# Conformer layer on one core: a sixth channel tile convolved by taps, statistics taken over pairs of tiles

## The chip, the core and the metric

The kernel runs on one NeuronCore of a Trainium2 chip. The core has TensorE (PE; its weight loads are listed apart as PEld), VectorE (DVE), ScalarE (ACT), GpSimd (POOL) and SyncE (SP, which here issues every transfer). Each engine works through a queue of its own in order; between engines there are only semaphores. The metric is the device time of one execution in microseconds.

## The reference, cut to what matters

A trunk of two layers over 512 positions and 1024 channels, all in float32. Layer 0 mixes by a gated DeltaNet, layer 1 by a Conformer convolution; both then attend to a memory of 256 positions and end in a squared-ReLU MLP. The change touches layer 1's mixer:

```python
def conformer_conv(h, w_pw1, b_pw1, w_dw, b_dw, ln_g, ln_b, w_pw2, b_pw2):
    u = h @ w_pw1 + b_pw1
    u = u[..., :D_MODEL] * jax.nn.sigmoid(u[..., D_MODEL:])
    c = causal_depthwise_conv(u, w_dw) + b_dw          # width 31, each channel by itself
    c = jax.nn.silu(layer_norm(c, ln_g, ln_b))         # mean and variance over the 1024 channels
    return c @ w_pw2 + b_pw2
```

`h` comes in after an RMS normalisation, and the result is added to the residual.

## The kernel before, in words

**Layout.** Activations lie with 128 channels on the partitions and 512 positions along the row: eight channel tiles, m = 0 to 7. Products are made at float32 precision from three matmuls: each operand is split into a high part (rounded by a copy on ScalarE) and the rest (a subtraction).

**Weights.** They come in units of 128 x 1024 (`raw`, loaded by SP into one of three buffers). `wsplit` casts a unit on ScalarE (`wh`, L207) and subtracts (`wl`, L70) on VectorE, or on GpSimd for all of pw1 and for every other unit of this layer's K and V. The split pair has three buffers, so the cast of unit u waits until TensorE is done with unit u - 3. In the Conformer layer I number the units: 0 to 15 are pw1 (two for each channel tile), 16 to 31 the K and V projections of the memory for the attention that follows (placed here as filler for TensorE, with their own high and low parts `Kh`, `Kl`, `Vh`, `Vl` and the scaled `kf`), 32 on pw2. Each unit of pw1 and pw2 is 24 matmuls of 128x512, each of K 24 of 128x256, each of V 12 of 128x512.

**Gate.** For each tile m, `pw_ev` scales the two halves of pw1's result by the RMS factor (`sg`, `pa` on VectorE), takes the sigmoid on ScalarE, and multiplies: `xp` for tile 0, `x` for tiles 1 to 4, `glu` for tiles 5 to 7.

**Convolution, in three ways.** In the program before:
- tile 0 by taps on GpSimd and ScalarE (`pool_conv`): for each of 31 taps ScalarE makes the product with the tap's weight (`cvp`, one or two instructions, L1052 and L1054, since positions are stored by phase of four) and GpSimd adds it to the accumulator (`ca<-ca,cvp`);
- tiles 1 to 4 by taps on VectorE (`dve_conv`): one multiply-add per tap on an accumulator in PSUM (`ca<-x,prm,ca`, 30 for each tile), after which ScalarE copies the accumulator to SBUF (L1072);
- tiles 5, 6 and 7 on TensorE (`conv`): the gated tile is rearranged by 16 small transfers on SP (`xg`), and 36 matmuls against nine prepared matrices of diagonals (`tap`, loaded by `taps`) give the result with positions on the partitions; VectorE adds it to `cy`, which holds the bias.

Tiles convolved by taps are turned by four transposes on TensorE (`turn`, `cvT`) and copied to `Y` (`cy`) by ScalarE.

**Normalisation.** `bn_stats` on VectorE takes the statistics of every tile and row block (32 instructions, of the transposes' PSUM or of `cy`), `bn_aggr` joins them, ScalarE takes the root, VectorE the reciprocal and the scaling of the eight `cy` tiles (L79). `ln_out` turns each tile back (`lnT`, four transposes), applies Silu on ScalarE (`la`) and splits it (`lsh` on ScalarE, `lsl` on VectorE). pw2 follows.

**Order.** `CONV_SEQ` lists the 32 units; behind each, some taps are taken from the lists of VectorE and GpSimd (`taps_dve`, `taps_pool`), and `CONV_AFTER` names what follows which unit: "t" loads diagonals, "c" convolves on TensorE, "d" turns a tile, "l" normalises, "o" writes a tile out. What the loop records is then ordered by a scheduler, engine by engine, so an instruction can stand elsewhere in its queue than the loop alone says; the order that results is fixed when the program is built, and can be read from it.

Of the kernel before, what the change touches and what calls it, by code (L numbers as in the profile page):

```python
# [8 lines left out]
F32 = mybir.dt.float32  # L9
F32R = mybir.dt.float32r  # L10
AF = mybir.ActivationFunctionType
ALU = mybir.AluOpType
# [1 line left out]

P = 128
NT = 512
NTAP = 5
KT = 8
EPS = 1e-6
LN_EPS = 1e-5  # L20
# [9 lines left out]
OFF["w_tap"] = _o  # L30
_o += NTAP * 31
OFF["out_norm"] = _o
# [6 lines left out]
def tile_trunk(ctx, tc, xT, memT, prm_d, adt_d, bdw_d, tap_d, fin_d, w_ab, w_kq, w_v, w_z, w_dno, w_pw1, w_pw2,  # L39
               w_q, w_k, w_vv, w_o, w_up, w_dn, yT):  # L40
    nc = tc.nc
    pe, act, dve, pool = nc.tensor, nc.scalar, nc.vector, nc.gpsimd
# [2 lines left out]
    wp = ctx.enter_context(tc.tile_pool(name="wp", bufs=2))  # L45
    fsp = ctx.enter_context(tc.tile_pool(name="fsp", bufs=3))
    up = ctx.enter_context(tc.tile_pool(name="up", bufs=NSLOT))
    sp = ctx.enter_context(tc.tile_pool(name="sp", bufs=13))
    psp = ctx.enter_context(tc.tile_pool(name="psp", bufs=8, space=bass.MemoryType.PSUM))

    cnt = [0]
# [5 lines left out]
    def slot(dt=F32, s="u", shape=(P, NT)):  # L57
        return up.tile(list(shape), dt, tag="u", name=nm(s))
# [7 lines left out]
    def const(shape, s, dt=F32):  # L66
        return cp.tile(list(shape), dt, tag=s, name=s)
# [67 lines left out]
    eps_ln = const([P, 1], "eps_ln")  # L135
# [128 lines left out]
    def split(src, s):  # L264
        h = slot(F32R, s + "h")
        act.copy(h, src)
        lo = slot(F32R, s + "l")
        tt(dve, lo, src, h.bitcast(F32), ALU.subtract)
        return h, lo
# [721 lines left out]
    def taps(m):  # L991

        TAPS[m] = []
        for i in range(9):
            t = slot(s="tap")
            nc.sync.dma_start(out=t, in_=tap_d[m - NTAP, i])
            TAPS[m].append(t)

    def conformer(norm, hres, nxt):
        xs = norm.xs  # L1000
        st, xg = {}, {}
        bn = slot(s="bn")
        Y = [[slot(s="cy") for _ in range(2)] for _ in range(4)]
# [7 lines left out]
        def pw_ev(m):  # L1011
            sg = slot(s="sg")
            tt(dve, sg, st.pop((m, 1)), norm.rb, ALU.mult)
            act.activation(sg, sg, AF.Sigmoid, bias=pc("b_pw1", 8 + m))
            a = slot(s="pa")
            tt(dve, a, st.pop((m, 0)), norm.rb, ALU.mult)
            if m == 0:
                x4 = c4(wp.tile([P, 544], F32, tag="cv", name=nm("xp"), bufs=NCV))
                pool.memset(x4[:, :, 0:8], 0.0)
                stt(x4[:, :, 8:136], c4(a), pc("b_pw1", m), c4(sg), ALU.add, ALU.mult)  # L1020
                todo_p.extend(pool_conv(m, x4))
                return
            if m < NTAP:
                x7 = fsp.tile([P, 1024], F32, tag="fs", name=nm("x7"))[:, 0:1008].rearrange("p (q t) -> p q t", q=7)
                pool.memset(x7[:, :, 0:10], 0.0)
                stt(x7[:, 3:7, 8:136], c4(a), pc("b_pw1", m), c4(sg), ALU.add, ALU.mult)
                act.copy(x7[:, 0:3, 9:137], x7[:, 4:7, 8:136])
                todo.extend(dve_conv(m, x7))
                return
            x = wp.tile([P, 544], F32, tag="cv", name=nm("xg"), bufs=NCV)  # L1030
            x4 = c4(x)
            pool.memset(x4[:, :, 0:8], 0.0)
            gl = slot(s="glu")
            stt(gl, a, pc("b_pw1", m), sg, ALU.add, ALU.mult)
            for j in range(4):
                for b in range(4):
                    nc.sync.dma_start(out=x4[32 * b:32 * b + 32, j, 8:136],
                                      in_=gl[32 * j:32 * j + 32, 128 * b:128 * b + 128])
            xg[m] = x4

        todo, todo_p, acc = [], [], {}
# [17 lines left out]
        def dve_conv(m, x7):  # L1059
# [13 lines left out]

            return [lambda d=d: tap(d) for d in range(31)]

        def taps_pool(n):
            for _ in range(min(len(todo_p), n)):
                todo_p.pop(0)()

        def taps_dve(us):  # L1080
            for _ in range(min(len(todo), round(us * TAP_RATE))):
                todo.pop(0)()

        def turn(m):
            ps = psum("cvT")
            for r in range(4):
                pe.transpose(ps[:, r * P:(r + 1) * P], acc[m][:, r * P:(r + 1) * P], ident)
            del acc[m]
            for r in range(4):
                y = ps[:, r * P:(r + 1) * P]  # L1090
                act.copy(Y[r][m // 4][:, m % 4 * P:m % 4 * P + P], y)
                dve.bn_stats(out=bn[:, (r * 8 + m) * 6:(r * 8 + m) * 6 + 6], in_=y)

        def conv(m, js):
            if js[0] == 0:
                st["cv", m] = psum("cv")
            ps = st["cv", m]
            for j in js:
                o = ps[:, j * P:(j + 1) * P]
                for u in range(9):  # L1100
                    x = xg[m][:, j, 8 - u:136 - u]
                    if u < 8:
                        pe.matmul(o, x, TAPS[m][2 * j + u // 4][:, (u % 4) * P:(u % 4 + 1) * P],
                                  start=u == 0, stop=False)
                    else:
                        pe.matmul(o[:, 0:64], x, TAPS[m][8][:, j * P:j * P + 64], start=False, stop=True)
            if js[-1] == 3:
                del TAPS[m], xg[m]
                ps = st.pop(("cv", m)).rearrange("p (j r c) -> p j r c", j=4, r=4)
                for r in range(4):  # L1110
                    y = Y[r][m // 4][:, m % 4 * P:m % 4 * P + P]
                    y3 = y.rearrange("p (j c) -> p j c", j=4)
                    tt(dve, y3, ps[:, :, r, :], y3, ALU.add)
                    dve.bn_stats(out=bn[:, (r * 8 + m) * 6:(r * 8 + m) * 6 + 6], in_=y)

        def ln():
            mv = small(8, "mv")
            for r in range(4):
                dve.bn_aggr(out=mv[:, 2 * r:2 * r + 2], in_=bn[:, r * 48:r * 48 + 48])
            v = mv.rearrange("p (r k) -> p r k", k=2)  # L1120
            sd = small(4, "lsd")
            act.activation(sd, v[:, :, 1], AF.Sqrt, bias=eps_ln)
            rs = small(4, "lrs")
            dve.reciprocal(rs, sd)
            for r in range(4):
                for y in Y[r]:
                    ts(dve, y, y, mv[:, 2 * r:2 * r + 1], ALU.subtract, rs[:, r:r + 1], ALU.mult)

        ss = []

        def ln_out(m):
            ps = psum("lnT")
            for r in range(4):
                pe.transpose(ps[:, r * P:(r + 1) * P], Y[r][m // 4][:, m % 4 * P:m % 4 * P + P], ident)
            a = slot(s="la")
            act.activation(a, ps, AF.Silu, scale=pc("ln_g", m), bias=pc("ln_b", m))
            ss.append(split(a, "ls"))


        after = {}  # L1140
        for i, what in CONV_AFTER:
            after.setdefault(i, []).append(what)
        for i, (kind, u) in enumerate(CONV_SEQ):
            if kind == "p":
                m, hf = divmod(u, 2)
                pw_mm(m, hf)
                if (m, hf) == (0, 0):
                    norm.stat()
                if (m, hf) == (0, 1):
                    norm.spread()  # L1150
                if hf == 1:
                    pw_ev(m)
            else:
                kv_unit(1, u)
            taps_dve(5.4 if kind == "p" else 2.8)
            taps_pool(2 if kind == "p" else 1)
            for what, m, *js in after.pop(i, ()):
                {"t": taps, "c": lambda m: conv(m, js), "l": lambda m: ln(), "o": ln_out, "d": turn}[what](m)
                taps_dve({"c": 2.0 * len(js)}.get(what, 0.0))
                taps_pool(3 if what == "c" else 0)  # L1160
        assert not after
        new = []
        for m in range(8):
# [84 lines left out]
    for gq in range(2):  # L1248
# [17 lines left out]
        n = 0  # L1266
# [51 lines left out]
    n3 = Norm("cv_norm")  # L1318
    h = mlp(0, n2, h, n3, lambda: (mem_gain(1, 0), mem_gain(1, 1), taps(NTAP)))
    n4 = Norm("xa_norm1")  # L1320
# [14 lines left out]
    def finish(hid, cur):  # L1335
# [3 lines left out]
        for c, g in LAST:  # L1339
# [14 lines left out]
            if g == 0:  # L1354
# [41 lines left out]
MLP_ORDER = [("up", 0), ("up", 1), ("dn", 0), ("up", 2), ("dn", 1), ("up", 3), ("dn", 2), ("dn", 3)]  # L1396
TAP_RATE = 1.1
CONV_SEQ = [("p", i) for i in range(16)] + [("k", i) for i in range(16)]
CONV_AFTER = [(3, ("t", 6)), (11, ("d", 1)), (13, ("c", 5, 0, 1, 2, 3)), (13, ("t", 7)), (15, ("c", 6, 0, 1, 2, 3)),
              (16, ("d", 2)), (17, ("c", 7, 0, 1, 2, 3)), (19, ("d", 0)), (23, ("d", 3)), (27, ("d", 4)), (27, ("l", 0))]  # L1400
CONV_AFTER += [(_i, ("o", _m)) for _m, _i in enumerate((29, 29, 30, 30, 30, 31, 31, 31))]


def _tiles_a(np, w):
# [18 lines left out]
def _taps(np, w):  # L1423
# [11 lines left out]
    e = np.concatenate([e[:, :, :, 0:8].reshape(128, 8, 128), e[:, :, :, 8].reshape(128, 8, 16)], axis=2)  # L1435
    e = e.reshape(4, 32, 8, 9, 16)[:, :, NTAP:]
    t = np.zeros((8 - NTAP, 9, 4, 32, 16, 32), w.dtype)
    for c in range(32):
# [60 lines left out]
```

## Time and profile before

| | |
|---|---|
| Median of three runs | 1555.77 us (1555.08 to 1556.25) |
| Profiled execution | 1555.59 us, its span 1553.8 us |
| First pw1 matmul of the Conformer layer | 863.0 us from the span's start |
| First matmul on diagonals | 943.5 us |
| First matmul of K, first of V | 971.6 us, 1004.0 us |
| First `lnT` transpose | 1026.7 us |
| First pw2 matmul | 1034.9 us |
| Taps on VectorE | 120, 892.2 to 1015.5 us, median 751 ns |
| Taps on GpSimd | 30, 881.3 to 968.4 us, median 1294 ns |

The page is read from the top: how busy each engine is, the chain of work that ended last, and the costliest groups of instructions. For the layer that is changed, the busy time by stretch, the waits of one engine, and the instructions in order of time are asked of the trace. A row of the timeline gives the start, the duration, the engine, the line, the operation, the tiles written and read, and in brackets the idle time ahead of it with what ended it. TensorE's rows overlap: a 128x512 matmul is listed with some 0.39 us, and the next starts 0.23 us later.

### The profile page before, as it was taken

The numbers are of one execution on the slowest core, as the hardware profiler recorded it, in microseconds if no ns is written. First come the engines' busy times: TensorE is split into PE (matmuls) and PEld (weight loads), VectorE is DVE, ScalarE is ACT, GpSimd is POOL, SyncE is SP. The second block draws the span as 40 slices with busy tenths as digits, with TensorE's granted clock in tenths as the row PEclk, the third lists the DMA queues.
The fourth block names the chain that finished last, engine by engine and source line by source line (L and its number), as shares of the span: only waits on it lengthen the run. The fifth ranks groups of instructions, "written<-read, shape, count | busy, mean of one in ns | idle before, by whom it ended". The sixth has DMA issues, their size and how long they took to land.

```text
span 1553.8 us, 19346 instructions
## 1 busy us (share of the span) xinstructions
PE 1519.2 (98%) x7560; PEld 1277.0 (82%) x7560; DVE 902.6 (58%) x1354; ACT 682.6 (44%) x1092; POOL 226.4 (15%) x231
## 2 busy tenths in 40 slices
PE   9999996999999999999999999989999999999998
PEld 7888885988888888888888888978888888888887
DVE  6798888676555444343435499975455443444441
ACT  6847654554444443231424454374444432322332
POOL 1311212001212000000001687212112000000000
PEclk9999997999999999999999999999999999999999
DMA  5122121352221222322224444333213223222231
GB/s 183 55 85 66 64 76 51 105 194 69 82 69 68 95 96 95 99 103 97 96 95 156 121 145 144 129 123 109 80 33 113 87 100 103 95 95 95 96 108 54
DMA packets 48475, 152.51 MB, mean 98 GB/s; under 512 B 6144, under 2 KB 7936, under 8 KB 48384
## 3 DMA queue, kind: packets, MB, share of 16 engines
q1 hardware_dynamic: 48384, 151.28, 29.2%
q8 instruction: 59, 0.97, 0.2%
q14 instruction: 32, 0.26, 0.1%
HBM read 148.37 MB, written 2.10 MB: 97 GB/s over the span
## 4 chain that ended last, share of the span: by engine, by line
PE 88%; DVE 7%; issue 2%; ACT 1%; SPq 1%; DMA 0%; POOL 0%; DVEq 0%; ACTq 0%; POOLq 0%
PE up L229 7%; PE up L230 7%; PE up L231 7%; PE dn L229 7%; PE dn L231 7%; PE dn L230 7%; PE h L230 2%; PE h L229 2%; DVE ca L73 2%; PE h L231 2%; PE q L229 2%; PE xo L230 2%; PE q L231 2%; PE xo L229 2%; PE q L230 2%
## 5 line engine op out<-in xcount | busy, mean ns | idle before, releaser
L207 ACT CAST wh<-raw 128x1024 fp32r<-128x1024 f32 x248 | 260.3, 1051 | 653.0 <-PE dn L230 190.4
L70 DVE TENSOR_TENSOR wl<-raw,wh 128x1024 fp32r<-128x1024 f32 x224 | 275.7, 1232 | 96.9 <-ACT wh L207 95.9
L229 PE MATMUL up<-xh,wh 128*128 128x512 f32 x512 | 200.2, 391 | 0.0
L231 PE MATMUL up<-xh,wl 128*128 128x512 f32 x512 | 199.2, 389 | 0.0
L230 PE MATMUL up<-xl,wh 128*128 128x512 f32 x512 | 199.2, 389 | 0.0
L231 PE MATMUL dn<-uh,wl 128*128 128x512 f32 x448 | 174.3, 389 | 0.0
L229 PE MATMUL dn<-uh,wh 128*128 128x512 f32 x448 | 174.3, 389 | 0.0
L230 PE MATMUL dn<-ul,wh 128*128 128x512 f32 x448 | 174.3, 389 | 0.0
L70 DVE TENSOR_TENSOR h<-dn,h 128x512 f32<-128x512 f32 x56 | 41.8, 747 | 163.2 <-PE dn L231 163.2
L73 DVE SCALAR_TENSOR_TENSOR rl<-up,rb 128x512 f32<-128x512 f32 x64 | 44.2, 691 | 156.7 <-PE up L231 156.7
L70 POOL TENSOR_TENSOR sq<-sq,sq 128x512 f32<-128x512 f32 x30 | 48.7, 1623 | 466.5 <-ACT sq L304 466.5
L229 PEld LDWEIGHTS up<-xh,wh 128*128 128x128 f32 x512 | 96.1, 188 | 20.3 <-issue 0.5
L230 PEld LDWEIGHTS up<-xl,wh 128*128 128x128 f32 x512 | 96.1, 188 | 20.3 <-issue 0.5
L231 PEld LDWEIGHTS up<-xh,wl 128*128 128x128 f32 x512 | 96.1, 188 | 20.1
L231 PEld LDWEIGHTS dn<-uh,wl 128*128 128x128 f32 x448 | 84.1, 188 | 17.5
L230 PEld LDWEIGHTS dn<-ul,wh 128*128 128x128 f32 x448 | 84.1, 188 | 17.4
L229 PEld LDWEIGHTS dn<-uh,wh 128*128 128x128 f32 x448 | 84.1, 188 | 17.4
L73 DVE SCALAR_TENSOR_TENSOR ca<-x,prm,ca 128x512 f32<-128x512 f32 x120 | 87.7, 749 | 3.0 <-ACT ca L1066 1.3
L229 PE MATMUL h<-xh,wh 128*128 128x512 f32 x192 | 79.9, 416 | 1.4 <-ACT xh L297 1.4
L230 PE MATMUL h<-xl,wh 128*128 128x512 f32 x192 | 77.5, 404 | 0.6 <-DVE xl L73 0.6
L231 PE MATMUL h<-xh,wl 128*128 128x512 f32 x192 | 77.5, 404 | 0.0
L70 POOL TENSOR_TENSOR wl<-raw,wh 128x1024 fp32r<-128x1024 f32 x24 | 58.7, 2448 | 53.5 <-ACT wh L207 53.5
(341 smaller groups left out, 3076.0 us busy)
## 6 DMA issues: line engine op xcount, KB each, us to landing
raw<-w_up SPq DMA_DIRECT2D x64, 512.0 KB, 3.5
raw<-w_dn SPq DMA_DIRECT2D x64, 512.0 KB, 3.6
raw<-w_pw SPq DMA_DIRECT2D x24, 512.0 KB, 3.7
raw<-w_kq SPq DMA_DIRECT2D x16, 512.0 KB, 3.7
raw<-w_k SPq DMA_DIRECT2D x16, 512.0 KB, 3.6
raw<-w_vv SPq DMA_DIRECT2D x16, 512.0 KB, 3.6
raw<-w_q SPq DMA_DIRECT2D x16, 512.0 KB, 3.4
raw<-w_o SPq DMA_DIRECT2D x16, 512.0 KB, 3.6
```

The lines of the kernel that those rows point to most:

```text
L70: return e.tensor_tensor(out=o, in0=a, in1=b, op=op)
L73: dve.scalar_tensor_tensor(out=o, in0=a, scalar=s, in1=b, op0=op0, op1=op1)
L207: ins = [act.copy(h, raw)]
L229: pe.matmul(ps, wh, xh, start=first, stop=False)
L230: pe.matmul(ps, wh, xl, start=False, stop=False)
L231: pe.matmul(ps, wl, xh, start=False, stop=last)
```

## The change

Tile 5 leaves TensorE and joins tile 0 as a tile by taps on GpSimd and ScalarE. The list of GpSimd's taps is drawn on at a fractional rate (`RATE_P`). The statistics are taken from `cy` for two tiles at once, sixteen instructions of 256 columns, when both tiles of a pair are there. A root of a constant is placed on ScalarE ahead of the normalisation (`ln_table`, step "s"), and every second Silu result is split wholly on VectorE. The places of the turns, of the diagonals' load and of the normalisation in `CONV_AFTER` change; the pool of small buffers goes from 13 to 12.

```diff
-NTAP = 5
+NTAP = 6
+PTAP = (0, 5)
...
-    sp = ctx.enter_context(tc.tile_pool(name="sp", bufs=13))
+    sp = ctx.enter_context(tc.tile_pool(name="sp", bufs=12))
...
-            if m == 0:
+            if m in PTAP:
                 x4 = c4(wp.tile([P, 544], F32, tag="cv", name=nm("xp"), bufs=NCV))
...
+        pace = [0.0]
+
         def taps_pool(n):
-            for _ in range(min(len(todo_p), n)):
+            pace[0] += n if todo_p else 0.0
+            while todo_p and pace[0] >= 1.0:
                 todo_p.pop(0)()
+                pace[0] -= 1.0
...
+        turned = set()
+
+        def moments(m):
+            turned.add(m)
+            if m ^ 1 in turned:
+                q = m // 2
+                for r in range(4):
+                    dve.bn_stats(out=bn[:, (r * 4 + q) * 6:(r * 4 + q) * 6 + 6],
+                                 in_=Y[r][q // 2][:, q % 2 * 256:q % 2 * 256 + 256])
...
                 act.copy(Y[r][m // 4][:, m % 4 * P:m % 4 * P + P], y)
-                dve.bn_stats(out=bn[:, (r * 8 + m) * 6:(r * 8 + m) * 6 + 6], in_=y)
+            moments(m)
...
                     tt(dve, y3, ps[:, :, r, :], y3, ALU.add)
-                    dve.bn_stats(out=bn[:, (r * 8 + m) * 6:(r * 8 + m) * 6 + 6], in_=y)
+                moments(m)
+
+        def ln_table():
+            tc.keep_in_program_order(act.activation(small(1), eps_ln, AF.Sqrt))
...
-                dve.bn_aggr(out=mv[:, 2 * r:2 * r + 2], in_=bn[:, r * 48:r * 48 + 48])
+                dve.bn_aggr(out=mv[:, 2 * r:2 * r + 2], in_=bn[:, r * 24:r * 24 + 24])
...
-            ss.append(split(a, "ls"))
+            if m % 2 == 0:
+                ss.append(split(a, "ls"))
+                return
+            lh, ll = slot(F32R, "lsh"), slot(F32R, "lsl")
+            dve.tensor_copy(lh, a)
+            tt(dve, ll, a, lh.bitcast(F32), ALU.subtract)
+            ss.append((lh, ll))
...
-            taps_pool(2 if kind == "p" else 1)
+            taps_pool(RATE_P[0] if kind == "p" else RATE_P[1] if u < 8 else RATE_P[2])
...
-                taps_pool(3 if what == "c" else 0)
+                taps_pool(RATE_P[3] if what == "c" else 0)
...
-CONV_AFTER = [(3, ("t", 6)), (11, ("d", 1)), (13, ("c", 5, 0, 1, 2, 3)), (13, ("t", 7)), (15, ("c", 6, 0, 1, 2, 3)),
-              (16, ("d", 2)), (17, ("c", 7, 0, 1, 2, 3)), (19, ("d", 0)), (23, ("d", 3)), (27, ("d", 4)), (27, ("l", 0))]
-CONV_AFTER += [(_i, ("o", _m)) for _m, _i in enumerate((29, 29, 30, 30, 30, 31, 31, 31))]
+RATE_P = (2.3, 1.2, 2.0, 5.5)
+CONV_AFTER = [(3, ("t", 6)), (11, ("d", 1)), (11, ("t", 7)), (15, ("c", 6, 0, 1, 2, 3)), (16, ("d", 2)), (18, ("d", 0)),
+              (18, ("c", 7, 0, 1, 2, 3)), (23, ("d", 3)), (28, ("s", 0)), (29, ("d", 4)), (29, ("d", 5)), (29, ("l", 0))]
+CONV_AFTER += [(_i, ("o", _m)) for _m, _i in enumerate((30, 30, 31, 31, 31, 31, 31, 31))]
```

A line outside the diff follows `NTAP`: the MLP of layer 0 calls `taps(NTAP)` in its middle, which before loads tile 5's diagonals and after loads tile 6's.

More of the change, by code (lines that the diff above doesn't have):

```diff
@@ L1155, in conformer @@
             taps_dve(5.4 if kind == "p" else 2.8)
-            taps_pool(2 if kind == "p" else 1)
+            taps_pool(RATE_P[0] if kind == "p" else RATE_P[1] if u < 8 else RATE_P[2])
             for what, m, *js in after.pop(i, ()):
-                {"t": taps, "c": lambda m: conv(m, js), "l": lambda m: ln(), "o": ln_out, "d": turn}[what](m)
+                {"t": taps, "c": lambda m: conv(m, js), "l": lambda m: ln(), "s": lambda m: ln_table(), "o": ln_out, "d": turn}[what](m)
                 taps_dve({"c": 2.0 * len(js)}.get(what, 0.0))
-                taps_pool(3 if what == "c" else 0)
+                taps_pool(RATE_P[3] if what == "c" else 0)
         assert not after
```

## The prediction

> **What bounds the kernel now.** I read the page's engine totals and its chain first, then the busy times by stretch of the Conformer layer, then what TensorE waits for there.
>
> ```profile
> span 1553.8 us, 19346 instructions
> PE 1519.2 (98%) x7560; PEld 1277.0 (82%) x7560; DVE 902.6 (58%) x1354; ACT 682.6 (44%) x1092; POOL 226.4 (15%) x231
> PE 88%; DVE 7%; issue 2%; ACT 1%; SPq 1%; DMA 0%; POOL 0%; DVEq 0%; ACTq 0%; POOLq 0%
> ```
>
> ```profile
> 934.00:964.00 30.00, 27.72 (x159) 23.91 (x157) 28.62 (x47) 13.16 (x27) 20.99 (x13) 1.00 0.34 104
> 964.00:1012.00 48.00, 48.00 (x382) 46.63 (x381) 45.78 (x84) 18.78 (x33) 16.00 (x8) 1.00 0.48 166
> 1012.00:1036.00 24.00, 20.02 (x103) 15.71 (x102) 20.32 (x33) 16.80 (x24) 3.89 (x2) 1.00 0.52 168
> ```
>
> ```profile
> PE cv L1103 <- DMA xg<-glu: 2.3, 3, 1.6
> PE cvT L1087 <- ACT ca L1072: 1.8, 1, 1.8
> PE lnT L1134 <- ACT la L1136: 1.5, 1, 1.5
> ```
>
> TensorE is the chain nearly everywhere. In the stretches (columns: span, PE, PEld, DVE, ACT, POOL busy) it loses 2.3 us at 934 to 964 and 4.0 at 1012 to 1036. What is special here is VectorE: 28.6 of 30 and 45.8 of 48 us busy. So the layer has two nearly full engines, and ScalarE and GpSimd, which get the new work, have room on average (18.8 and 16.0 of 48 us). Averages don't say whether the room lies where the order wants it.
>
> **TensorE's part.** Tile 5 loses 36 matmuls on the diagonals, and gains four transposes (`cvT`).
>
> ```profile
> 963.59 0.23 PE pw L231
> 963.83 1.79 PE cv L1103 x16
> 965.78 1.84 PE cv L1103 x16
> ...
> 969.80 1.84 PE cv L1103 x16
> 974.74 0.44 PE cvT L1087 x4
> ...
> 1030.80 0.39 PE L262 MATMUL V<-wh,ml 128*128 128x512 f32 x1
> ...
> 1034.89 0.50 PE L229 MATMUL pw<-lsh,wh 128*128 128x512 f32 x1 [0.67 <-ACT la L1136]
> ```
>
> One such tile costs four steps of 2.0 (963.83 to 971.8), 8.0 us. The last V matmul starts at 1030.8 and ends its place at 1031.0. Off this go tile 5's 8.0, about 1.3 of the wait for its `xg`, the 1.8 before `cvT`, and 2.5 us of the normalisation's transposes, which now stand behind all V; 0.4 comes on. If nothing else stopped TensorE, V would be done at 1031.0 - 13.6 + 0.4 = 1017.8. pw2 starts at 1034.9 before; from there 192 matmuls and everything behind are the same in both programs, so **the change is worth the shift of that start**.
>
> **The new tile on GpSimd and ScalarE.** 30 sums on GpSimd, up to two products each on ScalarE.
>
> ```profile
> L70 POOL TENSOR_TENSOR ca<-ca,cvp x30: 1267/1294/1742, 881.3 to 968.4; 128x512 f32<-128x512 f32 x30
> L1052 ACT ACTIVATE cvp<-xp,prm x30: 386/556/727, 880.3 to 965.4; 128x384 f32<-128x384 f32 x8, 128x256 f32<-128x256 f32 x8, 128x128 f32<-128x128 f32 x7, 128x512 f32<-128x512 f32 x7
> L70 DVE TENSOR_TENSOR wl<-raw,wh x10: 1210/1224/1241, 959.3 to 1029.7; 128x1024 fp32r<-128x1024 f32 x10
> L70 POOL TENSOR_TENSOR wl<-raw,wh x7: 2357/2404/2592, 964.8 to 1016.3; 128x1024 fp32r<-128x1024 f32 x7
> ...
> 981.23 0.58 ACT L1072 COPY ca<-ca 128x512 f32<-128x512 f32 x1 [0.39 <-DVE ca L73]
> ```
>
> 30 x 1.29 = 39 us of GpSimd and some 53 products, about 28 us of ScalarE. They would fit as sums. They don't fit as queued. In the changed program's order GpSimd does nine sums of tile 5 and the split (`wl`) of unit 20, eight sums, split 22, two sums, splits 24 and 26, six sums, splits 28 and 30, five sums. (Units are half weight tiles: 0 to 15 pw1, 16 to 31 K and V; the even ones of K and V are split here.) And ScalarE's order has, ahead of the products of the tenth sum, the copy of tile 3's accumulator (`ca`), which waits for VectorE's last tap of tile 3: what is queued behind that wait is GpSimd's food. That copy ran at 981.2 before. VectorE's load up to there hardly changes, so I put tile 3's end at 982.3 (one more unit split at 1.2 us, the sums of the statistics later). GpSimd: split 18 needs the buffer of unit 15, whose last matmul was at 963.6 before and is 9.3 earlier now, 954.3; with four sums of tile 0, ScalarE's cast and the split itself it is done near 960. Nine sums and split 20 (11.6 + 2.4, and two holds as below) end by about 976; then GpSimd stands idle some 7 us. From there:
>
> - copy 0.5 and two products 0.5 each: sums go on at 983.8; eight take 10.3, split 22 takes 2.4: 996.5.
> - TensorE without tile 5 wants unit 22 at 988.8 (a K or V unit is 24 matmuls of half width or 12 of full, 2.8 us: from 954.3 two tiles on diagonals 16.0, three units 8.4, two transposes 0.9 and 0.8 of waiting for `xg` end at 980.4, three more units at 988.8). It waits some 7 us, where it waited for nothing before.
> - Units 22 and 23 end at 1002.1. Split 26 needs ScalarE's cast (1.05 in the page's costliest group), which needs the buffer of unit 23: 1003.2, split done 1005.6. Six sums and split 28: 1005.6 + 7.7 + 2.4 = 1015.7.
> - Units 27 and 28 are interleaved, so TensorE stands in 27 until split 28 is there; 60 matmuls at 0.233 are left: 14.0 + 0.4. The transposes of tile 5, the last, start at **1030.1**. GpSimd's last five sums (6.5) and split 30 are done by then.
>
> **The port that VectorE and GpSimd share.**
>
> ```profile
> 904.22 0.75 DVE L73 SCALAR_TENSOR_TENSOR x<-pa,prm,sg 128x512 f32<-128x512 f32 x1
> ...
> 934.76 1.80 DVE L73 SCALAR_TENSOR_TENSOR glu<-pa,prm,sg 128x512 f32<-128x512 f32 x1
> ...
> 933.60 5.23 POOL L70 TENSOR_TENSOR wl<-raw,wh 128x1024 fp32r<-128x1024 f32 x2
> ...
> 889.18 1.75 DVE L73 SCALAR_TENSOR_TENSOR x<-pa,prm,sg 128x512 f32<-128x512 f32 x1 [0.86 <-ACT sg L1014]
> 890.34 3.13 POOL L70 TENSOR_TENSOR ca<-ca,cvp 128x512 f32<-128x512 f32 x2
> ```
>
> The same form takes VectorE 0.75 us, or 1.8 when it begins inside a GpSimd instruction: `glu` ends at 936.56, some 0.55 behind the first of the two splits (936.0). GpSimd pays too: two splits 5.23 instead of 4.8, two sums 3.13 instead of 2.6 next to `x`. The taps (`ca`, accumulator in PSUM) keep 0.75 throughout. So what takes both inputs from SBUF excludes GpSimd's work. After tile 3, GpSimd works through, and VectorE has `wl` of units 21, 23, 25, 27 and three `Kl` in its way before split 28: 4 x 1.2 + 3 x 0.6 = 6.6 us at most, of which I let 5.2 fall on GpSimd's chain: 1035.3.
>
> The Trainium skill, SBUF — State Buffer, § SBUF: two separate sides, says this as an exclusive lock: a VectorE instruction with two SBUF inputs and a GpSimd instruction that reads SBUF block each other for the whole instruction. The rows above agree, to the 0.55 us. By that rule the sum is 1035.3, without it 1030.1; it speaks against moving work onto GpSimd beside a full VectorE.
>
> **The tail.**
>
> ```profile
> L1091 ACT COPY cy<-cvT x4: 253/265/266, 1017.6 to 1023.0; 128x128 f32<-128x128 f32 x4
> ...
> 1023.63 0.37 DVE L1119 BATCH_NORM_AGGREGATE mv<-bn 128x2 f32<-128x48 f32 x1
> ...
> 1024.23 1.28 ACT L1122 ACT_TABLE_LOAD   x1
> 1026.07 3.74 DVE L79 TENSOR_SCALAR cy<-cy,mv,lrs 128x512 f32<-128x512 f32 x8
> 1029.78 0.78 ACT L1136 ACTIVATE la<-lnT,prm 128x512 f32<-128x512 f32 x1 [1.54 <-PE lnT L1134]
> 1034.07 0.77 ACT L1136 ACTIVATE la<-lnT,prm 128x512 f32<-128x512 f32 x1
> ```
>
> Before, V matmuls covered most of it. Now all V stand ahead of tile 5's transposes. From their start: 0.7 to the first copy, four copies 0.8, the last of the four sums over pairs 0.4, four aggregates 1.2 (3.1); root 0.4, its table ahead; a `wl` that stands on VectorE before the reciprocal ends at 4.3; reciprocal 0.2; seven of eight scalings 3.2 (7.7); transposes 0.4: first Silu at 8.1. pw2's first bank comes free when `Vl` is written, behind Silu, copy, Silu, `Vh` on ScalarE and one `Vl` on VectorE, 4.0: **12.1**. The table saves 1.3 less what the `wl` takes back. Splits half on VectorE: ScalarE then gives a tile per 1.1 us instead of 1.33, TensorE takes 1.4 for two banks; worth nothing. Statistics by pairs: sixteen instructions fewer on VectorE, and the four copies no longer alternate with them (1017.6 to 1023.0 before, 0.8 now); that is in the terms above.
>
> **Edits at nothing.** 13 to 12 small buffers: nothing in the waits there. The mid-MLP load of diagonals now fetches tile 6's, which step 3 of the layer fetches again: nine transfers of 256 KB at under half busy queues. Sixteen `xg` transfers of tile 5 go; they stood ahead of tile 6's on SP, which now follow two weight loads. If these loads came late, TensorE would wait in tile 6 as it did 2.3 us in all before; I keep 0.8 for it.
>
> **Idle TensorE.**
>
> ```profile
> 244.88 1.87 PE L762 MATMUL mssq<-ones,msq 128*128 128x1 f32 x8 [5.82 <-POOL msq L70]
> 247.18 0.63 PE L230 MATMUL h<-xl,wh 128*128 128x512 f32 x1
> 251.01 0.63 PE L230 MATMUL h<-xl,wh 128*128 128x512 f32 x1
> ...
> 262.11 1.19 PE L772 MATMUL mrs<-mdg,ones 128*128 128x256 f32 x2 [7.36 <-DVE mdg L70]
> ```
>
> After waits of 5.8 and 7.4 us matmuls came every 0.43 us instead of 0.23 (nine from 247.18 to 251.01): twelve times, and seven times after the second, 2.4 and 1.4 us. The change makes three such waits: before unit 22, in unit 27, before pw2. That is 0 (gaps split up) to 6 us; I take 2.
>
> The Trainium skill, TensorE: Matmul & The Clock Gate, § What's actually happening, has the same: half clock after an idle window of about 3.4 us. By its rule every one of the three costs; without it the forecast would be 2 us lower.
>
> **Sum.** 1030.1 with no holds and full clock, 1035.3 with holds; VectorE's tile 3 may end 3 us earlier or later. I take 1033 for the last transposes, plus 12.1 is 1045.1, plus 2 is 1047. Against 1034.9: +12. The profiled execution took 1555.6 (span 1553.8), 0.2 below the median 1555.8: **1567.6**. Its own range: 1560 (tile 3 three us earlier, no holds, full clock: +4.3) to 1575 (holds, three later, clock: +19).
>
> **Rivals.**
> - TensorE leads after all: if the tile's products aren't held (tile 3 ends by about 970 on VectorE, or ScalarE meets the copy later), the splits come in time, V ends at 1017.8 and pw2 starts at 1029.9: 5 us faster, 1550.6. For it: ScalarE and GpSimd are idle over half of 964 to 1012. Against: the order of the queues. It decides from last transposes earlier than 1022.8.
> - Even: GpSimd's sum alone bounds: 983.8 + 21 x 1.29 + 5 x 2.4 = 1022.9 with no wait of splits for TensorE's buffers, plus 12.1: 1035, no change. Against: splits stand behind sums.
> - VectorE bounds, and GpSimd's chain doesn't:
>
> ```profile
> 1015.51 0.77 DVE ca L73
> ```
>
> Tile 4's last tap ran at 1015.5. Twelve instructions with two SBUF inputs (eight `wl`, four `Kl`), each held half a sum, 0.65, put it at 1023.3; copy 0.6 and the 14 V matmuls that stand between the two last transposes, 3.3: 1027.2, pw2 at 1039.3, +4.4: slower, 1560. For it: VectorE is full at 964 to 1012, and nearly as many instructions stand in its queue as before. Against: GpSimd's chain ends later still.
>
> **How the numbers follow.** A change under 0.2% (3.1 us) can't be told here. The forecast 0.65; VectorE's bound 0.10, slower as well; even 0.10; TensorE leading 0.15. Slower 0.75, same 0.10, faster 0.15. From 1554 to 1576 I hold the forecast, VectorE's bound and most of the even case, 0.8.
>
> **What would show it.** Right: GpSimd idle some 7 us near 976 to 984, released by ScalarE's `cvp`; TensorE waiting on GpSimd's `wl` before unit 22 and in 27; `wl` on VectorE at 2 us; no V under `lnT`; TensorE's clock below 1 near 1000. Wrong: GpSimd's sums without a gap, V done before 1020.

## The result, and the profile after

The changed kernel takes 1578.1 us against 1555.4 us of the kernel before: a ratio of 1.0144, 95% interval 1.0126 to 1.0161, so 22.7 us slower. The forecast was 1567.6 with a range of 1554 to 1576. The direction came out, and most of the order of events; the size did not: the time lies 10.5 us above the forecast and 2.1 above the range.

The page of the changed kernel:

```profile
span 1577.4 us, 19271 instructions
PE 1521.2 (96%) x7492; PEld 1277.7 (81%) x7492; DVE 904.6 (57%) x1338; ACT 704.4 (45%) x1147; POOL 271.1 (17%) x261
PE 88%; DVE 6%; issue 2%; POOL 2%; ACT 1%; DMA 0%; SPq 0%; POOLq 0%; DVEq 0%; ACTq 0%
```

The span is 23.6 us longer, and TensorE has 68 rows fewer yet 2 us more of busy time. (A matmul of the convolution stands twice in the trace: tile 5's 36 make 72 rows, and four transposes come on.) GpSimd, with 0% of the chain before, now has 2% of it. What TensorE waits for longest in the Conformer layer (total, times, longest):

```profile
PE K L232 <- POOL wl L71: 7.2, 1, 7.2
PE V L262 <- POOL wl L71: 6.5, 1, 6.5
PE lnT L1152 <- DVE cy L80: 4.1, 1, 4.1
PE cvT L1102 <- POOL ca L71: 3.4, 1, 3.4
PE cv L1118 <- DMA xg<-glu: 3.2, 1, 3.2
```

Before, the longest were 2.3 us (three waits together), 1.8 and 1.5. Now two are for a split that GpSimd makes (units 22 and 28), one is for its last sum, one is the uncovered tail, one is for tile 6's copies. GpSimd's own queue in order of time (start, duration, what, count, idle time ahead):

```profile
961.45 13.61 POOL L71 TENSOR_TENSOR ca<-ca,cvp 128x512 f32<-128x512 f32 x9
976.03 2.41 POOL L71 TENSOR_TENSOR wl<-raw,wh 128x1024 fp32r<-128x1024 f32 x1 [0.96 <-ACT wh L208]
987.80 13.13 POOL L71 TENSOR_TENSOR ca<-ca,cvp 128x512 f32<-128x512 f32 x8 [9.37 <-ACT cvp L1055]
1000.89 2.34 POOL L71 TENSOR_TENSOR wl<-raw,wh 128x1024 fp32r<-128x1024 f32 x1
...
1012.16 2.42 POOL L71 TENSOR_TENSOR wl<-raw,wh 128x1024 fp32r<-128x1024 f32 x1 [4.01 <-ACT wh L208]
1014.52 10.18 POOL L71 TENSOR_TENSOR ca<-ca,cvp 128x512 f32<-128x512 f32 x6
1024.66 2.34 POOL L71 TENSOR_TENSOR wl<-raw,wh 128x1024 fp32r<-128x1024 f32 x1
...
1039.35 6.72 POOL L71 TENSOR_TENSOR ca<-ca,cvp 128x512 f32<-128x512 f32 x5 [3.54 <-ACT cvp L1055]
```

Here the forecast can be laid beside the trace. GpSimd stands idle for 9.4 us until the first product behind the copy of tile 3's accumulator; then eight sums, the split of unit 22, and TensorE, which waited 7.2 us for it, goes on at 1003.3. The split of unit 28 (1024.66) stands behind six sums. The last five sums end at 1046.07, and the last transposes wait for them:

```profile
1046.13 1.12 PE L1102 MATMUL cvT<-ident,ca 128*128 128x128 f32 x4 [3.37 <-POOL ca L71]
```

On ScalarE:

```profile
986.26 0.59 ACT L1073 COPY ca<-ca 128x512 f32<-128x512 f32 x1 [6.77 <-DVE ca L74]
...
1032.29 1.05 ACT L208 CAST wh<-raw 128x1024 fp32r<-128x1024 f32 x1 [11.46 <-PE V L263]
...
1036.86 1.06 ACT L208 CAST wh<-raw 128x1024 fp32r<-128x1024 f32 x1 [1.06 <-PE V L263]
1037.82 0.57 ACT L1073 COPY ca<-ca 128x512 f32<-128x512 f32 x1
1038.30 0.51 ACT L1053 ACTIVATE cvp<-xp,prm 128x256 f32<-128x256 f32 x1
```

The products for the last five sums begin at 1038.3: they stand behind casts of later weight units, which wait for V to free a buffer, and behind the copy of tile 4's accumulator. The clock, in stretches (span, PE, PEld, DVE, ACT, POOL, clock):

```profile
994.00:1000.00 6.00, 2.13 (x18) 1.93 (x17) 5.96 (x9) 3.89 (x7) 5.69 (x5) 1.00 0.24 85
1000.00:1006.00 6.00, 2.72 (x12) 2.72 (x13) 0.39 (x1) 0.00 (x0) 5.92 (x5) 0.59 0.23 57
...
1024.00:1030.00 6.00, 2.94 (x7) 2.36 (x8) 4.02 (x6) 0.00 (x0) 3.01 (x2) 0.58 0.30 88
...
1048.00:1054.00 6.00, 2.69 (x12) 2.15 (x12) 5.96 (x18) 2.58 (x4) 0.00 (x0) 0.50 0.55 175
```

Behind each long wait the granted clock is near a half.

### The profile page after: what moved, and what is told of

Same layout as the page of the kernel before. It is cut to its first block, busy times and chain, and to the rows that moved or that the text cites. A ratio compares the mean times of both kernels' runs of the same rounds, so it can differ in the third digit from the quotient of the medians.

```text
span 1577.4 us, 19271 instructions
## 1 busy us (share of the span) xinstructions
PE 1521.2 (96%) x7492; PEld 1277.7 (81%) x7492; DVE 904.6 (57%) x1338; ACT 704.4 (45%) x1147; POOL 271.1 (17%) x261
## 4 chain that ended last, share of the span: by engine, by line
PE 88%; DVE 6%; issue 2%; POOL 2%; ACT 1%; DMA 0%; SPq 0%; POOLq 0%; DVEq 0%; ACTq 0%
PE up L230 7%; PE up L231 7%; PE up L232 7%; PE dn L231 6%; PE dn L230 6%; PE dn L232 6%; PE pw L230 2%; PE pw L231 2%; PE pw L232 2%; PE h L230 2%; PE h L231 2%; PE h L232 2%; PE q L230 2%; PE xo L231 2%; PE q L232 2%
## 5 line engine op out<-in xcount | busy, mean ns | idle before, releaser
L71 POOL TENSOR_TENSOR ca<-ca,cvp 128x512 f32<-128x512 f32 x60 | 84.8, 1414 | 23.6 <-ACT cvp L1055 19.1
```

Of the source, the lines that this page charges most:

```text
L71: return e.tensor_tensor(out=o, in0=a, in1=b, op=op)
```

## Experiments

The theory: tile 5 carries the loss, through the order of the queues (splits behind sums on GpSimd, products behind waiting casts and copies on ScalarE), with VectorE held by GpSimd's sums and a tail that no V matmul covers any more. Rivals: the smaller edits have a part; the sums are simply too long; the tail alone; VectorE's own taps.

Times are medians; the marks are read from each trace as start plus duration, in us from the span's start. The last transposes are `cvT`; the start of pw2 moves with the layer's end. Each ratio is to runs of the kernel before on the same chip, whose medians lay between 1555.4 and 1556.6.

| kernel | us | ratio to before, 95% | VectorE's last tap | GpSimd's last sum | last transposes | pw2 |
|---|---|---|---|---|---|---|
| before | 1555.4 | 1 | 1016.3 | 970.0 | 1016.9 | 1034.9 |
| after | 1578.1 | 1.0126 to 1.0161 | 1037.7 | 1046.1 | 1046.1 | 1058.6 |
| all but tile 5 | 1556.1 | 0.9989 to 1.0007 | 1015.5 | 970.9 | 1017.4 | 1036.7 |
| tile 5 alone | 1579.0 | 1.0137 to 1.0165 | 1034.4 | 1044.1 | 1044.2 | 1057.4 |
| K, V splits on VectorE | 1568.0 | 1.0068 to 1.0095 | 1026.2 | 1034.5 | 1034.6 | 1047.1 |
| copies on VectorE | 1572.6 | 1.0096 to 1.0123 | 1032.6 | 1041.2 | 1041.2 | 1053.1 |
| both | 1569.8 | 1.0075 to 1.0105 | 1028.3 | 1037.6 | 1037.7 | 1050.2 |
| both, sums early | 1563.0 | 1.0030 to 1.0060 | 1027.1 | 1025.0 | 1029.1 | 1042.6 |
| both, steeper still | 1563.5 | 1.0035 to 1.0065 | 1028.1 | 1018.3 | 1030.6 | 1043.9 |
| sums early alone | 1572.3 | 1.0092 to 1.0120 | 1031.5 | 1025.8 | 1036.1 | 1049.9 |
| no sums of tile 5 but the first | 1560.9 | 1.0020 to 1.0043 | 1021.9 | 961.9 | 1023.2 | 1040.5 |
| tile 6 one unit later | 1577.6 | 1.0120 to 1.0154 | 1037.2 | 1045.5 | 1045.6 | 1058.0 |

### Which part of the change

Everything but tile 5:

```diff
-NTAP = 6
-PTAP = (0, 5)
+NTAP = 5
+PTAP = (0,)
...
-RATE_P = (2.3, 1.2, 2.0, 5.5)
+RATE_P = (2, 1, 1, 3)
```

`CONV_AFTER` is again that of the kernel before, with ("s", 0) behind unit 26.

> The changed kernel with tile 5 back on TensorE (NTAP 5, PTAP (0,), the order lists of before); the statistics by pairs, root's table ahead, half of the last splits on VectorE and the pool of 12 buffers stay. Theory (the loss of 22.7 us comes from tile 5's sums on GpSimd and its products on ScalarE, and from the tail that they leave uncovered): without tile 5 the rest costs nothing; the wait of the first scaled transposes is gone or no longer than before, and the time is 1551 to 1556 us, against 1555.4 of the kernel before. Rival (the smaller edits have a part in it, by VectorE's holds or by the smaller pool): 1558 us or more.

Tile 5 alone (`RATE_P`, `CONV_AFTER` and the pool of 12 buffers of the changed kernel, the rest as before; shown against the changed kernel, cut):

```diff
-            moments(m)
+                dve.bn_stats(out=bn[:, (r * 8 + m) * 6:(r * 8 + m) * 6 + 6], in_=y)
...
-            if m % 2 == 0:
-                ss.append(split(a, "ls"))
-                return
...
-(28, ("s", 0)),
```

> The kernel before with tile 5's convolution by taps alone, its rates and order list as in the changed kernel; statistics by single tiles, root's table where it was, the last splits all as before. Theory (tile 5 carries the loss): 1576 to 1582 us, the waits of TensorE for GpSimd's parts of w (7.2 and 6.5 us) and for the accumulator of tile 5 (3.4 us) stand as in the changed kernel, and the tail is some 2 us longer by the table and the moments. Rival (the parts act together): under 1572 us.

The first takes 0.9998 of the time before, the second 1.0151: tile 5 carries the whole loss, and statistics by pairs, the root's table and the Silu results split on VectorE are worth nothing that can be measured. The second kernel's waits are placed otherwise than I expected:

```profile
PE cv L1108 <- DMA xg<-glu: 7.9, 1, 7.9
PE cvT L1092 <- POOL ca L71: 6.9, 1, 6.9
PE lnT L1139 <- DVE cy L80: 4.7, 1, 4.7
PE K L232 <- POOL wl L71: 3.8, 1, 3.8
PE V L262 <- POOL wl L71: 2.9, 1, 2.9
```

More is waited for tile 6's transfers at the start, so less for the splits and again more for the last sum: the same end by other stops. A wait by itself says little about its worth here.

### The order on GpSimd and on ScalarE

All lower parts of K's and V's weights on VectorE:

```diff
-        gp = kind == "pw1" or j and kind in "KV" and i == 1 and hf == 0
+        gp = kind == "pw1"
```

> The changed kernel with the eight lower parts of w for K and V, which GpSimd made behind its sums, made on VectorE as all the others are. Theory (queue order on GpSimd): the two waits of TensorE for GpSimd (7.2 and 6.5 us) and the lower clock behind them go, tile 5's 30 sums run without a break, and the time is 1557 to 1567 us; what is left above the kernel before is the uncovered tail from the last transposes to the next stage, 12.5 us, less the matmuls that tile 5 no longer needs. Rival (the sums by themselves, 30 of 1.29 us and their holds of VectorE, set the end): the last sum ends no more than 3 us earlier, and the time is 1573 us or more.

The copies of the accumulators on VectorE:

```diff
-                    act.copy(acc[m], st.pop("ca"))
+                    dve.tensor_copy(acc[m], st.pop("ca"))
```

> The changed kernel with the copies of the tiles' accumulators made on VectorE, not on ScalarE, so that ScalarE's products for tile 5 don't stand behind a copy that waits for VectorE's taps. Theory (ScalarE held by that copy from about 977 to 986 us into the span): GpSimd's sums resume near 978, its idle 9.4 us shrink to under 3, the parts of w behind the sums come some 7 us earlier, and the time is 1566 to 1573 us. Rival (ScalarE's hold is covered, and only the splits' place counts): 1576 to 1580 us.

Splits off GpSimd: 1568.0, 10 us less (the end of the expected range was missed by one; the sums did not run without a break, they stood idle for 12.4 and 14.2 us). Copies off ScalarE: 1572.6, 5.5 us less, as expected; there the sums go on behind an idle time of 2.1 us:

```profile
978.94 10.82 POOL L71 TENSOR_TENSOR ca<-ca,cvp 128x512 f32<-128x512 f32 x8 [2.06 <-ACT cvp L1055]
```

So both orders cost. Both edits at once:

> Both edits at once: all lower parts of w for K and V and the copies of the tiles' accumulators on VectorE. Theory (queue order on GpSimd and on ScalarE, two separate costs): GpSimd's idle of 12.4 us in the kernel with the splits moved alone goes, the sums run from 958 to about 1000 us but for the last five, whose products still stand behind the last casts of w; 1562 to 1567 us, under the 1568.0 of the splits alone. Rival (VectorE, 139 of 150 us busy from 900 to 1050 in the kernel with the splits moved, sets the end by tile 4's last tap): 1567 to 1571 us, GpSimd done earlier and nothing gained.

1569.8: they don't add up. The rival's number came, but not its reason: the last transposes waited 4.2 us for GpSimd's last sum, not for VectorE's last tap (1028.3). GpSimd, first, and ScalarE of this kernel:

```profile
988.59 20.46 POOL L71 TENSOR_TENSOR ca<-ca,cvp 128x512 f32<-128x512 f32 x12 [16.54 <-ACT cvp L1055]
1009.41 6.66 POOL L71 TENSOR_TENSOR ca<-ca,cvp 128x512 f32<-128x512 f32 x4 [0.36 <-ACT cvp L1055]
1029.65 7.99 POOL L71 TENSOR_TENSOR ca<-ca,cvp 128x512 f32<-128x512 f32 x5 [13.59 <-ACT cvp L1055]
```

```profile
983.75 1.05 ACT L208 CAST wh<-raw 128x1024 fp32r<-128x1024 f32 x1 [5.58 <-issue]
986.59 1.05 ACT L208 CAST wh<-raw 128x1024 fp32r<-128x1024 f32 x1 [1.78 <-PE K L231]
987.54 0.51 ACT L1053 ACTIVATE cvp<-xp,prm 128x256 f32<-128x256 f32 x1
```

GpSimd's idle time did not go, it grew to 16.5 us: with the copy gone, the next products stand behind casts. The second of them waits for TensorE to free a weight buffer; for the first the profile names nothing. And the last five sums still wait 13.6 us. What delays the sums is what stands ahead of their products in ScalarE's queue, and the copy is only one such thing.

### The step that failed

The prediction had the last five sums done in time. Issuing more sums per unit moves their products ahead of the last casts, with both edits and alone:

```diff
-RATE_P = (2.3, 1.2, 2.0, 5.5)
+RATE_P = (2.3, 1.8, 3.0, 5.5)
```

> As the kernel with both edits, and with more sums of tile 5 issued per unit (RATE_P 2.3, 1.8, 3.0, 5.5), so that all 30 products stand ahead of the last casts of w on ScalarE. Theory (the prediction's failed step: the last five sums came 13 us late because their products stand behind casts that wait for V): the last sum ends before 1010 us, the wait of TensorE for tile 5's accumulator (3.9 us) goes, the last transposes wait for tile 4 on VectorE or for V alone, and the time is 1557 to 1563 us. Rival (VectorE's tile 4 sets the same end anyway): within 2 us of the kernel with both edits.

> The changed kernel with more sums of tile 5 issued per unit (RATE_P 2.3, 1.8, 3.0, 5.5) and nothing else: the last five products stand ahead of the last casts of w and of the copy of tile 4's accumulator on ScalarE; the splits for K and V stay on GpSimd, behind more sums each. Theory (the prediction's step "GpSimd's last five sums are done by then" is the one that failed; the copies hold the rest): the last sum ends at least 6 us earlier than 1046.1, TensorE no longer waits for tile 5's accumulator, but the last transposes then wait for tile 4, whose last tap ended at 1037.7: 1569 to 1573 us. Rival (more sums ahead of each split make TensorE wait longer for them, and what the tail gains is given back): 1575 to 1580 us.

With both edits the time falls from 1569.8 to 1563.0, alone from 1578.1 to 1572.3, both as expected (the last sum came at 1025.0, not before 1010). The wait for tile 5's accumulator is gone. For the single edit:

```profile
PE K L232 <- POOL wl L71: 9.2, 1, 9.2
PE V L262 <- POOL wl L71: 5.4, 3, 3.0
PE cv L1118 <- DMA xg<-glu: 4.5, 3, 3.2
```

TensorE waits longer for the split of unit 22 (9.2 instead of 7.2 us; the split itself is done at 1002.9, in the changed kernel at 1003.2), and the time is still 5.8 us less: the last sums no longer hold the end. Issuing them still earlier (4.0 per unit of K instead of 1.8) gives nothing more:

> The kernel with both edits, and the sums issued still earlier (RATE_P 2.3, 4.0, 3.0, 5.5): GpSimd's idle 15.2 us at 973 to 988, when the next products stand behind a cast of w that waits for TensorE to free its buffer, should shrink. Theory (GpSimd's last sum at 1025.0 comes down by what the idle loses, but tile 4 on VectorE, 1027.05, holds the end): within 2.5 us of 1563.0. Rival (GpSimd's chain leads, through its holds on VectorE too): 1556 to 1560 us.

1563.5: GpSimd is done 6.7 us earlier (1018.3) and the end does not move. GpSimd's last sum no longer leads there.

### Without the sums

```diff
-                tt(pool, a, a, b, ALU.add)
+                if m == 0 or d == 1:
+                    tt(pool, a, a, b, ALU.add)
```

> The changed kernel without GpSimd's sums of tile 5 but the first; the products on ScalarE stay. It leaves 29 of the 31 taps of one channel tile out of the result; its time shows what the sums cost by themselves and by the place they take in GpSimd's queue. Theory (the sums and what stands behind them are the loss, the tail is a part of it): no wait of TensorE for GpSimd's parts of w, VectorE's subtractions back at 1.22 us, 1558 to 1564 us. Rival (the tail that no V matmul covers is the main loss, 12 us): 1567 us or more.

1560.9, inside the theory's range, though a wait of 2.3 us and one of 0.9 for GpSimd's splits stay. So 17.2 of the 22.7 us are the sums and what they delay. The remaining 5.5 are not the sums'; the longest wait of TensorE is then the uncovered tail, 5.8 us for the scaled tiles (`cy`).

### Tile 3's lateness

Tile 6's convolution waited 3.2 us for its copies and then ran at half the clock, and VectorE waited for it. One unit later:

```diff
-(15, ("c", 6, 0, 1, 2, 3)), (16, ("d", 2)),
+(16, ("d", 2)), (16, ("c", 6, 0, 1, 2, 3)),
```

> The changed kernel with tile 6's convolution on TensorE one unit later, behind the first unit of K, so that its four copies through the queue of SP are in when it starts. Theory (tile 3's taps ended 4.0 us late because VectorE waited for tile 6, which waited 3.2 us for the copies and then ran at half the clock): TensorE's wait of 3.2 us and the lower clock behind it go, tile 3's last tap ends 2 to 4 us earlier, and the time is 1573 to 1577 us. Rival (tile 3 is set by VectorE's own work and the holds): 1577 to 1580 us.

The wait falls to 0.7 us and the time stays (1577.6), the rival's side: tile 3's copy comes at 985.3 instead of 986.3. What TensorE gains early it gives back in waits for splits of K, 4.6 us for GpSimd's and 4.3 for VectorE's, since the end hangs on other queues.

### Two chains that end together

In the kernel with both edits and early sums, VectorE's tile 4 (1027.1) and GpSimd's tile 5 (1025.0) end within 2 us. TensorE came to the last transposes out of V's matmuls, without a wait; before, it had waited 6.0 us in V and 3.3 in K for VectorE's subtractions. So VectorE's queue holds it by `wl` at least as much as by the last tap. I took VectorE to lead and left out half of tile 4's taps:

```diff
-                stt(a, src, w, a, ALU.mult, ALU.add)
+                if m < 4 or d % 2:
+                    stt(a, src, w, a, ALU.mult, ALU.add)
```

> The kernel with both edits and the early sums, with 15 of tile 4's 31 taps left out of the result (their instructions on VectorE are not issued): some 10 us less of work on VectorE between 1004 and 1027 us into the span, everything else as it was. Theory (VectorE's last tap, of tile 4, sets the last transposes, and the 12 to 13 us behind them follow): the last tap ends 7 to 10 us earlier, and the time falls from 1563.0 to 1553 to 1557 us. Rival (GpSimd's last sum, 1025.0, or the V matmuls set it as much): 1559 us or more.

1563.9, nothing gained: the theory fell. VectorE's last tap came at 1010.7, but:

```profile
PE cvT L1103 <- POOL ca L71: 7.1, 1, 7.1
PE V L261 <- ACT wh L208: 2.8, 1, 2.8
```

```profile
988.44 38.96 POOL L71 TENSOR_TENSOR ca<-ca,cvp 128x512 f32<-128x512 f32 x21 [14.81 <-ACT cvp L1055]
```

The 21 sums take 39 us there and end at 1027.4. Then the other two corners of the square, without the sums, with tile 4 whole and half:

> The kernel with both edits and the early sums, without GpSimd's sums of tile 5 but the first (29 taps of that tile are left out of the result); tile 4 whole on VectorE. With the half of tile 4 left out alone the time had stayed (1563.9 against 1563.0), because the transposes of tile 5 then waited 7.1 us for GpSimd's last sum, at 1027.4. Theory (two chains end within some 2 us of each other, VectorE's tile 4 and GpSimd's tile 5, and each alone holds the end): without the sums VectorE loses the holds (1.6 to 1.9 us against 1.22 in some ten subtractions, about 6 us) and tile 4 ends near 1021: 1555 to 1560 us. Rival (a third thing, the casts of w on ScalarE behind the products, sets the end): 1561 us or more.

> Both left out: 15 taps of tile 4 on VectorE and 29 sums of tile 5 on GpSimd; the products on ScalarE stay. Theory (the two chains set the end together): the last transposes come before 1018 us, the tail is covered by V's matmuls, TensorE has 14 us of matmuls less than in the kernel before, and the time is 1544 to 1552 us. Rival (ScalarE's 60 halves of products and the casts behind them, or the tail, hold the end by themselves): 1556 us or more.

| both edits, early | sums | no sums |
|---|---|---|
| tile 4 whole | 1563.0 | 1559.4 (1.0011 to 1.0031) |
| tile 4 half | 1563.9 (1.0037 to 1.0064) | 1552.7 (0.9972 to 0.9991) |

Half of tile 4 is worth nothing beside the sums and 6.7 us without them: two chains, VectorE's queue and GpSimd's, each of which holds the end alone. VectorE's subtractions (`wl`, shortest, median, longest in ns) of the kernel with the sums, and of the one without them, tile 4 whole in both:

```profile
L71 DVE TENSOR_TENSOR wl<-raw,wh x12: 1212/1634/2119, 986.4 to 1029.7; 128x1024 fp32r<-128x1024 f32 x12
```

```profile
L71 DVE TENSOR_TENSOR wl<-raw,wh x13: 1217/1219/1226, 985.0 to 1028.2; 128x1024 fp32r<-128x1024 f32 x13
```

The sums give the holds, some 0.4 us in each. The Trainium skill, SBUF — State Buffer, § SBUF: two separate sides, has VectorE with two SBUF inputs and GpSimd exclude each other for a whole instruction; these two rows agree.

Both chains out of the way, pw2 starts at 1030.5, 4.4 us earlier than before, and 2.8 us are gained. I expected 1552 at most. TensorE is then the chain, with one long wait of 2.9 us and its clock behind it. So with 29 sums and 15 taps left undone the spared matmuls bring 0.2%; in this order the room for a gain was small from the start.

### Another tile on GpSimd

Tile 4 in place of tile 5, so that VectorE loses a tile and TensorE keeps its three:

```diff
-PTAP = (0,)
+PTAP = (0, 4)
```

on the kernel with everything but tile 5, with splits and copies on VectorE and `RATE_P` 2.3, 1.8, 3.0, 5.5.

> Tile 4 instead of tile 5 by taps on GpSimd and ScalarE: tile 5 back on TensorE as in the kernel before, VectorE left with three tiles, all lower parts of w for K and V and the copies on VectorE, sums issued early. TensorE has the work of the kernel before and VectorE 30 taps of 0.66 us less. Theory (VectorE sets the end of this stage, TensorE's spared matmuls could not): the waits of TensorE in this stage in the kernel before (1.8 and 1.5 us behind the last tile and the statistics) go, the tail is covered by V's matmuls again, 1549 to 1554 us. Rival (30 more sums on GpSimd cost as much through VectorE's holds and late products as the taps did): 1556 to 1562 us.

1558.3, ratio 1.0011 (1.0002 to 1.0020): no gain, the rival's number. Of its two reasons the holds don't lead: VectorE has room (10.4 us of 20 busy at 980 to 1000, 19.1 before), GpSimd's sums end at 1019.0, and TensorE comes to the last transposes (1021.1) and to pw2 (1036.5, 1.6 us later than before) without a wait. What it waits for longest is ScalarE:

```profile
979.80 39.24 POOL L71 TENSOR_TENSOR ca<-ca,cvp 128x512 f32<-128x512 f32 x23 [7.93 <-ACT cvp L1053]
1000.36 0.39 PE L230 MATMUL K<-mh,wh 128*128 128x256 f32 x1 [2.37 <-ACT wh L208]
```

ScalarE works through its products without a break up to that cast (999.3), and behind the wait TensorE has half its clock from 1002.6 to 1006.0, some 1.7 us of its work.

> As the kernel with tile 4 on GpSimd, with half of the lower parts of w for K and V on GpSimd again as in the changed kernel, and the sums at an even rate (RATE_P 2, 1.5, 1.5, 3). It tells whether splits behind sums cost where VectorE and TensorE have room. Theory (a split behind sums comes late whatever tile is summed): a wait of TensorE for GpSimd's part of w shows again, and the time is 2 to 8 us above the kernel with the splits on VectorE. Rival (with the sums at an even rate they find their place): within 1 us of it or faster.

1567.2 (1.0058 to 1.0086). This run doesn't answer its question: at the even rate five of the 30 sums come behind the transposes, so five taps are left out of the result, and TensorE waited 11.4 us for the sums ahead of the transposes. It shows only that at this rate the sums come too late. None of the kernels with the whole computation beats the kernel before.

## Why the prediction was right and wrong

**Right.** Its order of events stands in the trace: GpSimd idle behind the copy of tile 3's accumulator, TensorE waiting about 7 us for unit 22 (7.2) and again inside 27 and 28 (6.5), `wl` on VectorE at up to 2 us (five of eleven at 1.45 to 2.15, all beside GpSimd's sums, the others at 1.17 to 1.31), no V under `lnT`, half the clock behind each long wait. That the first wait has the forecast's length is luck: TensorE came to unit 22 at 996.1 and not at 988.8, since it waited 3.2 us for tile 6's copies, where 0.8 was kept, and then convolved tile 6 at the lower clock in 10.8 us and not 8.0; and split 22 was done at 1003.2 and not at 996.5. "The change is worth the shift of that start": pw2 moved by 23.7 us, the span by 23.6. The tail, 12.1 forecast, is 12.5 (1046.1 to 1058.6). The edits at nothing are nothing (0.9998).

**The failed step** is "GpSimd's last five sums (6.5) and split 30 are done by then". It followed the sums through GpSimd's queue and not their products through ScalarE's, where they stand behind casts that wait for V (with the copies gone from ScalarE the last five sums still waited 6.0 us for them). The last transposes waited 3.4 us for them, a term that the sum put at nothing. Issuing the products earlier, and nothing else, took 5.8 us off; that is more than the 3.4, since other stops moved with it (in that run TensorE kept its full clock in tile 6's convolution).

**Mis-sized terms.** From 1030.1, the last transposes by the sum without holds, to the measured 1046.1:

- tile 3's end: the sums go on at 987.8, not 983.8: 4.0. "VectorE's load up to there hardly changes" allowed 1.1 over the 981.2 of before, and the copy came 5.0 later. Without the sums it comes at 984.0, 2.3 earlier, but in that run TensorE also kept its full clock in tile 6's convolution, and VectorE stood 1.0 us less behind it; so at most 1.3 are the sums' and some 1.0 tile 6's (with tile 6 one unit later the copy came 1.0 earlier). The other 1.7 I can't place;
- holds: eight sums took 13.13 instead of 10.3, six took 10.18 instead of 7.7: 5.3, just the 5.2 of the rule; I had taken some 2.9, a point between the two sums;
- the clock: units 22 and 23 at half clock put split 26 2.2 late, V's first matmuls another 1.3: 3.5 (2 taken, pw2's share included);
- the last sums: 3.4 (none taken).

Together 16.2, of 16.0 measured. Against the 1047 at which I put pw2, 4.0 + 2.4 + 1.5 + 3.4 + 0.4 of tail give 11.7, and it started at 1058.6, 11.6 later. All five terms went the same way; beside the failed step it is sizes that were off, not the mechanism. The range was too narrow by its own terms, too: its top, +19, took some 3.5 us for the clock, where the prediction had allowed up to 6; with 6 the top is 1577.

**The rivals.** Two prices came near, and the conditions weren't met. "TensorE leads" was priced at 1550.6 with pw2 at 1029.9; with both chains cut it is 1552.7 and 1030.5. "VectorE bounds" was priced at 1560 with the last tap at 1023.3; without the sums it is 1559.4 to 1560.9, the last tap at 1021.5 to 1021.9. That agreement is luck: the price came from holds by the sums, and these runs have no sums of tile 5 after the first. "Even: GpSimd's sum alone bounds" didn't show in any run: splits apart and sums early, VectorE and GpSimd end together, 7 us behind.

## What to carry to other kernels

Work that is moved to two idle engines as producer and consumer has to be followed through both queues: a consumer with room on average starves where the producer's instruction stands behind something that waits for a third engine. Before unloading the engine on the chain, ask how soon the next chains end; here VectorE and GpSimd stood right behind TensorE, so the 8 us of spared matmuls brought 2.8 even with both chains cut. Where a rule gives a full price for holds, take it whole: here 5.2 us were forecast by it and 5.3 measured, where 2.9 had been taken.

## What was not expected of the hardware

The length of a wait alone doesn't decide whether TensorE's clock drops. In the kernel with both chains cut, 2.9 us were enough:

```profile
995.96 0.73 PE L261 MATMUL V<-wh,mh 128*128 128x512 f32 x2 [2.90 <-ACT wh L208]
...
996.88 0.42 PE L231 MATMUL K<-ml,wh 128*128 128x256 f32 x1
997.09 0.42 PE L232 MATMUL K<-mh,wl 128*128 128x256 f32 x1
...
1000.06 0.28 PE L231 MATMUL K<-ml,wh 128*128 128x256 f32 x1
```

The matmuls of K then come every 0.21 us instead of 0.12, until 3.9 us after the wait's end. In the kernel with everything but tile 5 even 1.83 us were enough; the granted clock is 0.64 from 1026.6 to 1030.0:

```profile
1026.67 0.44 PE L1152 MATMUL lnT<-ident,cy 128*128 128x128 f32 x2 [1.83 <-DVE cy L80]
```

And the wait for tile 6's copies lowered the clock in the changed kernel, first row, but not in the one with the sums early alone, second row, where it was no shorter:

```profile
957.72 3.75 PE L1118 MATMUL cv<-tap,xg 128*128 128x128 f32 x16 [3.16 <-DMA xg<-glu]
```

```profile
956.55 2.02 PE L1118 MATMUL cv<-tap,xg 128*128 128x128 f32 x16 [3.25 <-DMA xg<-glu]
```

The Trainium skill, TensorE: Matmul & The Clock Gate, § What's actually happening, puts the drop behind an idle window of about 3.4 us, counted by windows that run freely. Windows that run freely would let one length fall out either way, as here; that TensorE must be idle for such a window does not fit the 1.83 and 2.90 us, and there the measurement decides.

And a GpSimd sum depends on what VectorE does beside it. Its median was 1.29 us in the kernel before. With both edits and early sums, the last 21 sums have a mean of 1.66 us beside tile 4's taps and the subtractions, and 1.78 with half of those taps gone. (They take 36.5 and 39.0 us, short gaps included.) Taking accumulations in PSUM off VectorE made GpSimd slower. In these stretches VectorE spends 17.9 of 36.5 us, and 23.1 of 38.9, on subtractions with two SBUF inputs (`wl`, `Kl`); that this share is the reason is argued, since no run varies it alone.
